# Subtract the row mean and square: stores issued from ScalarE's queue, and tiles of consecutive rows instead of interleaved ones

## The chip, the core and the metric

The kernel runs on one core of one Trainium2 chip. Of the core's engines it uses VectorE (DVE in the profile), ScalarE (ACT), SyncE (SP, which only issues transfers here) and the 16 DMA engines that move data between HBM and the on-chip memory (SBUF, 128 partitions). The metric is the device time of one execution in microseconds (us), as a median over runs.

## The reference

The input `x` is a float32 array of 1024 rows of 4096 elements; the axis is the last one.

```python
mean = np.mean(x, axis=axis, keepdims=True)
return ((x - mean) ** 2).astype(np.float32)
```

So every row is reduced to its mean, the mean is subtracted, and each element is squared. 16.78 MB are read and 16.78 MB are written.

## The kernel before

The work is cut into two tiles. A tile holds 512 rows: each of the 128 partitions holds four whole rows (`Q = 4`), 16,384 floats or 64 KiB, one row behind the other. Both tiles have a buffer of their own (`bufs=ntiles`), so no load waits for a buffer.

Which rows of `x` a partition holds is set by the rearrange pattern `"(p n q) d -> n p (q d)"`: partition `p` owns the eight consecutive rows `8p` to `8p+7`; tile 0 takes the first four of each partition's eight, tile 1 the last four. In HBM, the 64 KiB run of one partition in one tile therefore starts 128 KiB after that of the partition before it. The output is laid out in the same way.

All loads are issued first, on SP's queue (line 51): for tile 0 a short head of 512 columns and then the remaining 15,872 columns, for tile 1 one transfer of the whole tile.

Then the tiles are worked on one after the other, all in place in `x_tile`:

- ScalarE takes the mean of row 3 with an activation that also accumulates (line 59, `mean_on_act`), then the squares: row 3, row 0, row 1 and the first 2304 columns (`H`) of row 2 (line 74, `square_on_act`, with the negated mean as the bias).
- VectorE takes the means of rows 0, 1 and 2 (line 67 a reduction, line 70 the scaling by 1/4096), and then the last 1792 columns of row 2: an addition of the negated mean (line 89) and a multiplication with itself (line 90).
- One store of the whole tile (8 MiB) is issued at line 91, on SP's queue, where it waits for VectorE's line 90 and for ScalarE's last square.

`inorder` (`tc.keep_in_program_order`) pins an instruction behind what was traced before it on its engine. The reductions, the scalings and the squares are pinned in this way; the activation of line 59, the lines 89 and 90 and the transfers are not, and are placed by the scheduler of the tile framework from their data and their order in the program. Line 122 is the end of the program: SP waits there for all transfers.

Of the kernel before, what the change touches and what calls it, by code (L numbers as in the profile page):

```python
# [2 lines left out]

os.environ.setdefault("NEURON_RT_ULTRASERVER_MODE", "4")

# [4 lines left out]

F32 = mybir.dt.float32
ACT = mybir.ActivationFunctionType


@with_exitstack
def kernel(
    ctx: ExitStack,
    tc: tile.TileContext,
    x: bass.AP,
    axis: bass.AP,  # L20
    out: bass.AP,
):

    nc = tc.nc

    B, D = x.shape  # L30
    P = nc.NUM_PARTITIONS
    Q = 4
    HEAD = 512
    H = D * 9 // 16
    assert B % (P * Q) == 0
    ntiles = B // (P * Q)
    inv_d = 1.0 / float(D)

    x_t = x.rearrange("(p n q) d -> n p (q d)", p=P, q=Q)
    out_t = out.rearrange("(p n q) d -> n p (q d)", p=P, q=Q)  # L40

    io = ctx.enter_context(tc.tile_pool(name="io", bufs=ntiles))
    scratch = ctx.enter_context(tc.tile_pool(name="scratch", bufs=1))
    stats = ctx.enter_context(tc.tile_pool(name="stats", bufs=2 * ntiles * Q))

    tiles = []
    for i in range(ntiles):
        x_tile = io.tile([P, Q * D], F32)
        cuts = [0, HEAD, Q * D] if i == 0 else [0, Q * D]
        for lo, hi in zip(cuts, cuts[1:]):  # L50
            nc.sync.dma_start(out=x_tile[:, lo:hi], in_=x_t[i][:, lo:hi])  # L51
        tiles.append(x_tile)

    inorder = tc.keep_in_program_order

    def mean_on_act(row):
        copy = scratch.tile([P, D], F32)
        neg_mean = stats.tile([P, 1], F32)
        nc.scalar.activation(  # L59
            out=copy, in_=row, func=ACT.Identity, scale=-inv_d, accum_out=neg_mean  # L60
        )
        return neg_mean

    def mean_on_dve(row):
        neg_sum = stats.tile([P, 1], F32)
        neg_mean = stats.tile([P, 1], F32)
        inorder(nc.vector.reduce_sum(  # L67
            out=neg_sum, in_=row, axis=mybir.AxisListType.X, negate=True
        ))
        inorder(nc.vector.tensor_scalar_mul(out=neg_mean, in0=neg_sum, scalar1=inv_d))  # L70
        return neg_mean

    def square_on_act(part, neg_mean):
        inorder(nc.scalar.activation(  # L74
            out=part, in_=part, func=ACT.Square, bias=neg_mean, scale=1.0
        ))

    for i in range(ntiles):
        row = [tiles[i][:, q * D:(q + 1) * D] for q in range(Q)]
        m3 = mean_on_act(row[3])  # L80
        m0 = mean_on_dve(row[0])
        square_on_act(row[3], m3)
        m1 = mean_on_dve(row[1])
        square_on_act(row[0], m0)
        m2 = mean_on_dve(row[2])
        square_on_act(row[1], m1)
        square_on_act(row[2][:, :H], m2)
        back = row[2][:, H:]
        nc.vector.tensor_scalar_add(out=back, in0=back, scalar1=m2)  # L89
        nc.vector.tensor_mul(out=back, in0=back, in1=back)  # L90
        nc.sync.dma_start(out=out_t[i], in_=tiles[i])


# [1 line left out]
_INS = ['x', 'axis']  # L95
_OUTS = [((1024, 4096), 'float32')]

_NUMBERS = {'axis': -1}


# [26 lines left out]
```

## Time and profile before

| what | us |
|---|---|
| median of 3 runs | 83.14 |
| lowest and highest of them | 82.9 and 83.14 |
| the profiled execution's own time | 83.14 |
| its span in the profile | 81.4 |
| DVE busy | 33.4 |
| ACT busy | 34.7 |
| the 16 DMA engines busy, share of the span | 95.9% |

The span runs from the first to the last instruction of the profiled execution; what lies between the span and the execution's own time (83.14 - 81.4) is outside the profile. Busy times are summed over an engine's instructions. The share of the DMA engines is a mean over all 16 of them. The profile's queue `q1` is the one hardware queue that all five transfers of this kernel use, since all are issued from SP.

The traced transfers are cut into packets: 128 of 2 KiB (the head), 128 of 63,488 bytes (the rest of tile 0's load) and 384 of 64 KiB (tile 1's load and the two stores), and 80 of 4 bytes (one at the end of each of the five transfers on each of the 16 engines). Every large packet is one partition's run, so each DMA engine moves eight of them for each transfer.

### The profile page before, as it was taken

Reading aid. Unit: us, or ns where it says so; the run is one execution under the profiler, and the core shown is the slowest. Engines: PE = TensorE matmul, PEld = TensorE weight load, DVE = VectorE, ACT = ScalarE, POOL = GpSimd, SP = SyncE. Lnnn points to the kernel's source line nnn. Section 1 sums busy time; section 2 is a strip of 40 time slices with the busy share of each in tenths; the row PEclk is TensorE's granted clock in tenths of the full one; section 3 lists DMA queues with packets and bytes.
Section 4 is the critical chain, followed back from the end, with each engine's and each line's share of the span. In section 5 each row is a group of like instructions: output and inputs, shape, how many; then the busy total and the mean of one; then the engine's idle time right before and its main releaser. Section 6 shows DMA issues by size and latency. Waiting matters only on the chain.

```text
span 81.4 us, 83 instructions
## 1 busy us (share of the span) xinstructions
DVE 33.4 (41%) x16; ACT 34.7 (43%) x13; POOL 0.2 (0%) x4
## 2 busy tenths in 40 slices
DVE  0000000000089999999439999999900000000000
ACT  6000000000099999999339999999800000000000
POOL 0000000000000000000000000000000000000000
DMA  1999939999992999993899998399999199999290
GB/s 26 602 499 468 406 156 468 499 499 499 516 451 97 483 516 516 516 483 161 387 516 516 516 483 387 161 516 516 516 516 451 64 516 516 516 516 483 129 419 0
DMA packets 720, 33.55 MB, mean 412 GB/s; under 512 B 80, under 2 KB 80, under 8 KB 208
## 3 DMA queue, kind: packets, MB, share of 16 engines
q1 hardware_dynamic: 720, 33.55, 95.9%
HBM read 16.78 MB, written 16.78 MB: 412 GB/s over the span
## 4 chain that ended last, share of the span: by engine, by line
DMA 49%; DVE 21%; SPq 1%; issue 0%
DMA x_tile<-in_x_dram 49%; DVE neg_sum L67 16%; DVE x_tile L90 2%; DVE x_tile L89 1%; SPq L51 1%; DVE neg_mean L70 1%
## 5 line engine op out<-in xcount | busy, mean ns | idle before, releaser
L67 DVE TENSOR_REDUCE neg_sum<-x_tile 128x1 f32<-128x4096 f32 x6 | 26.5, 4412 | 25.0 <-DMA x_tile<-in_x_dram 25.0
L74 ACT ACTIVATE x_tile<-x_tile,neg_mean 128x4096 f32<-128x4096 f32 (+1 forms) x8 | 26.0, 3324 | 0.1
L59 ACT ACTIVATE copy<-x_tile 128x4096 f32<-128x4096 f32 x2 | 7.2, 3617 | 23.1 <-DMA x_tile<-in_x_dram 23.1
L90 DVE TENSOR_TENSOR x_tile<-x_tile 128x1792 f32<-128x1792 f32 x2 | 4.1, 2026 | 0.1
L89 DVE TENSOR_SCALAR x_tile<-x_tile,neg_mean 128x1792 f32<-128x1792 f32 x2 | 2.3, 1153 | 0.1
L59 ACT ACT_TABLE_LOAD x1 | 1.3, 1283 | 0.7 <-PEq L108 0.7
L70 DVE TENSOR_SCALAR neg_mean<-neg_sum 128x1 f32<-128x1 f32 x6 | 0.9, 154 | 0.2
L59 ACT ACTIVATION_READ_ACCUMULATOR copy<-x_tile 128x1 f32 x2 | 0.4, 186 | 0.0
L108 POOL MEMSET const-bfloat16-1.0<- 128x1 bf16 x1 | 0.1, 102 | 0.0
L108 POOL MEMSET const-uint8-127<- 128x1 uint8 x1 | 0.1, 101 | 0.0
L108 POOL MEMSET const-float32-0.0<- 128x1 f32 x1 | 0.1, 99 | 0.2 <-issue 0.2
L108 POOL MEMSET const-float32-1.0<- 128x1 f32 x1 | 0.1, 98 | 0.0
## 6 DMA issues: line engine op xcount, KB each, us to landing
x_tile<-in_x_dram SPq DMA_DIRECT2D x1, 7936.0 KB, 21.4
x_tile<-in_x_dram SPq DMA_DIRECT2D x1, 256.0 KB, 2.6
out_dram<-x_tile SPq DMA_DIRECT2D x2, 21.7
x_tile<-in_x_dram SPq DMA_DIRECT2D x1, 40.2
```

What stands on the lines that cost most here:

```text
L51: nc.sync.dma_start(out=x_tile[:, lo:hi], in_=x_t[i][:, lo:hi])
L59: nc.scalar.activation(out=copy, in_=row, func=ACT.Identity, scale=-inv_d, accum_out=neg_mean)
L67: inorder(nc.vector.reduce_sum(out=neg_sum, in_=row, axis=mybir.AxisListType.X, negate=True))
L70: inorder(nc.vector.tensor_scalar_mul(out=neg_mean, in0=neg_sum, scalar1=inv_d))
L74: inorder(nc.scalar.activation(out=part, in_=part, func=ACT.Square, bias=neg_mean, scale=1.0))
L89: nc.vector.tensor_scalar_add(out=back, in0=back, scalar1=m2)
L90: nc.vector.tensor_mul(out=back, in0=back, in1=back)
L108: nc = _bacc.Bacc("TRN2", target_bir_lowering=False, num_devices=1)
```

## The change

The rows that a partition owns are dealt out in another way, and the store is issued from another engine:

- In `"(n p q) d -> n p (q d)"` tile 0 is the first 512 rows of `x` and tile 1 the last 512. Partition `p` holds rows `4p` to `4p+3` of its tile, and the runs of neighbouring partitions follow each other in HBM without a gap: 64 KiB apart instead of 128 KiB. A whole tile is one block of 8 MiB. The output is laid out in the same way. Sizes and counts of transfers, the order of the loads, and what the engines compute stay as they are.
- The store of a tile is issued by `nc.scalar.dma_start`, on ScalarE's queue, instead of by `nc.sync.dma_start`. In the program it stands behind ScalarE's last square of that tile and ahead of its first activation of the next one. The loads stay on SP's queue.

An empty line falls away as well, so line numbers behind it are smaller by one in the new file.

```diff
@@ -24,7 +24,6 @@
-
     nc = tc.nc
...
-    x_t = x.rearrange("(p n q) d -> n p (q d)", p=P, q=Q)
-    out_t = out.rearrange("(p n q) d -> n p (q d)", p=P, q=Q)
+    x_t = x.rearrange("(n p q) d -> n p (q d)", p=P, q=Q)
+    out_t = out.rearrange("(n p q) d -> n p (q d)", p=P, q=Q)
...
         nc.vector.tensor_scalar_add(out=back, in0=back, scalar1=m2)
         nc.vector.tensor_mul(out=back, in0=back, in1=back)
-        nc.sync.dma_start(out=out_t[i], in_=tiles[i])
+        nc.scalar.dma_start(out=out_t[i], in_=tiles[i])
```

## The prediction

> **What bounds the kernel now.** I read the page's engine lines first, then its DMA lines, then the chain of waits, and then the timeline and the transfer windows around the two places where a store is issued. The page, busy times and DMA:
>
> ```profile
> DVE 33.4 (41%) x16; ACT 34.7 (43%) x13; POOL 0.2 (0%) x4
> q1 hardware_dynamic: 720, 33.55, 95.9%
> ```
>
> No compute engine is busy for half the span; the 16 DMA engines are for 95.9% of it. The chain of waits, in order of time, with the lines between left out:
>
> ```profile
> 1.64 40.24 DMA x_tile<-in_x_dram
> ...
> 56.76 2.02 DVE x_tile L90
> ```
>
> The chain runs through the loads to 41.88, through tile 1's computation to 58.78, and what is left of the span belongs to the last store: 21.7 us from its issue to its landing. That looks like load, compute, store in a row, but the DMA engines never rest meanwhile. Windows over the transfers show it. A packet is booked at its start, so GB/s times the length, divided by 65,536 bytes, is the number of 64 KiB packets that start in a window. The columns: window, length, DVE, ACT, POOL busy, clock, DMA share, GB/s.
>
> ```profile
> 38.30:39.20 0.90, 0.90 (x1) 0.90 (x1) 0.00 (x0) 1.00 2.70 1165
> 39.20:40.80 1.60, 0.30 (x1) 0.09 (x1) 0.00 (x0) 1.00 0.00 0
> 40.80:41.05 0.25, 0.00 (x0) 0.00 (x0) 0.00 (x0) 1.00 1.22 524
> 41.05:41.60 0.55, 0.00 (x0) 0.00 (x0) 0.00 (x0) 1.00 3.86 1668
> 41.60:43.20 1.60, 1.30 (x1) 1.30 (x1) 0.00 (x0) 1.00 0.00 0
> ...
> 60.30:60.90 0.60, 0.00 (x0) 0.00 (x0) 0.00 (x0) 1.00 4.05 1748
> ...
> 77.20:77.80 0.60, 0.00 (x0) 0.00 (x0) 0.00 (x0) 1.00 4.03 1748
> 77.80:80.30 2.50, 0.00 (x0) 0.00 (x0) 0.00 (x0) 1.00 0.00 0
> ```
>
> At 38.3 to 39.2 all 16 engines start their last packet of tile 1's load; at 40.8 to 41.6 (2 packets, then 14) they start the first of store 0; at 60.3 to 60.9 the first of store 1; at 77.2 to 77.8 the last of all. The trace's packet records give the rest. A 64 KiB packet takes 2.418 us in the median (27.1 GB/s on one engine), read or written, 2.487 at worst; a 63,488-byte one takes 2.342 us once the stream runs, but the first on each engine takes up to 2.994. The first packet starts at 1.74, the last ends at 80.21, and no engine stands idle for over 0.39 us in all between. One engine's load is 8 head packets (0.90 us, their mean sum), 8 x 2.342 and 24 x 2.418: 77.7 us, of the 78.5 there are. The DMA engines are the bound, and no reordering of the same bytes can take much from it. A change of over 0.3%, 0.25 us, is about what a measurement of this kernel can tell from none.
>
> **Part 1, the rows.** Removed and added: nothing in counts. The five transfers, their packets and their sizes stay; only HBM addresses move, from a pitch of 128 KiB to 64 KiB. The trace has no packet at the new pitch. The nearest rows are the 384 packets at the old one: reads and writes both at 2.418 us, so HBM isn't what limits a packet now, and I take zero. Above: if the packets of one direction all took the worst steady time, 2.487, that is 16 x 0.069 = +1.1 us; of both directions, +2.2 us. Below: steady packets show no stall that could go, but the start does. The engines come out of the head and their first large packet spread out, and that spread lasts to the end: in the last transfer the earliest engine ends at 79.67, the last at 80.21. If the new addresses let all start as the best do, -0.54 us.
>
> A rule weighed against that row stands in the Trainium skill, page "DMA: Bandwidth & Descriptors", section "Latency and other measured facts": copies with a large power-of-two pitch between the partitions' rows lose rate (207 GB/s per direction at 512 KiB, 103 at 4 MiB, 214 with a pad), and it advises contiguous tiles. Its smallest pitch is four times the one here; taken at its word for 512 KiB, the 3% between 207 and 214 would be an estimated gain of some 2.6 us and 80.5 us. The row of 2.418 us leaves no room for that.
>
> **Part 2, the store's queue.** Two DMA issues (0.35 us each on SP) go from SP's queue to ACT's, with their two waits on VectorE. Both issue places in the timeline:
>
> ```profile
> 37.47 2.03 DVE L90 TENSOR_TENSOR x_tile<-x_tile 128x1792 f32<-128x1792 f32 x1
> 39.56 0.35 SPq L91 DMA_DIRECT2D out_dram<-x_tile  x1
> 41.90 3.62 ACT L59 ACTIVATE copy<-x_tile 128x4096 f32<-128x4096 f32 x1 [2.61 <-DMA x_tile<-in_x_dram]
> ...
> 58.85 0.34 SPq L91 DMA_DIRECT2D out_dram<-x_tile  x1
> ```
>
> *The wait.* ACT ends its last square of tile 0 at 39.29, VectorE ends line 90 at 39.50. ACT now stands 0.2 us at the wait and issues at 39.56 as SP did. Behind it on ACT is tile 1's line 59, which waits for tile 1's load until 41.90 anyway: 41.90 - 39.56 - 0.35 = 2.0 us of cover. If the load landed earlier than that, each issue of 0.35 us would lie on ACT's path. In tile 1 nothing is queued behind the store but the end of the program, where SP waits for the landing as before. On SP nothing useful stood behind the stores. Cost: 0.
>
> *The start.* No issue from ACT is in this trace. From the issue to the first packet it took 41.04 - 39.56 = 1.48 us for the store, and 1.74 - 0.73 = 1.01 us for the first load, so one issue can differ from another by 0.47 us. How much of a delay shows? The engine that finishes last is free for store 0 at 41.58 and for store 1 at 60.90, while first packets can start at 41.04 and, at the same distance from the issue, at 60.33: 0.54 us of slack. Both stores shift alike, and store 1's issue doesn't depend on store 0, so a delay of d costs max(0, d - 0.54) once. For d I take 0 to 0.47, the nearest rows: cost 0. At the upper end a whole second start, 1.48 us, costs 0.94. An earlier start gains nothing, because the engines are still busy with the load.
>
> *The order between queues.* On one queue store 0's packets stood behind tile 1's load; on two queues nothing says so. But when the first store packet can start, at 41.04, each engine has long begun its last load packet (all between 38.3 and 39.2): there is none left to overtake. The margin is 41.04 - 39.2 = 1.8 us. If the store came earlier than that, one packet of it on every engine would push the load's landing by 2.42 us, and with it store 1's start from 60.33 to 62.75, behind the 60.90 at which the last engine falls free: +1.85 us.
>
> The rule that speaks against the change is on the same page of the skill, section "Queues, rings and completion order": each DMA engine takes turns between the queues that have work, packet by packet. This trace, with one queue, can't show it; by it, two queues cost 0 within that margin and the same 1.85 us outside it.
>
> **The sum.** Rows 0, wait 0, start 0, order 0. Against the profiled execution's own 83.14 us (span 81.4 and 1.7 around it), which is also the median of the runs shown: 83.1.
>
> **The rivals.**
>
> *ACT starts transfers later* (slower). For it: every issue in the trace is SP's, and 0.54 us is little. Against: issues differ by 0.47 at most here. It decides from d = 0.54 on; 0.79 is needed for 0.25 us; at d = 1.48, 84.1 us.
>
> *The 64 KiB pitch disturbs HBM* (slower). For it: first packets of up to 2.994 us show that packets can be held up. Against: 384 packets without a stall. One direction at the worst steady row: 83.14 + 1.1 = 84.2; both: 85.3.
>
> *Tile 1's mean goes ahead of store 0 on ACT* (slower). Line 59 isn't pinned by `inorder`, so the program doesn't force the store before it. Then ACT would stand at the load until 41.90 and issue no sooner: first packets at 41.90 + 1.48 = 43.38, 1.8 us after the last engine falls free, 84.9 us; if the issue also waits for the activation's end, 3.6 us more. Against: the store comes first in the program and its wait ends 2.4 us before the load lands.
>
> *A smoother start* (faster). For it: the spread of 0.54 us and a head that takes until 2.67 to 3.02. Against: nothing says that the new addresses do better. 82.6 us, and no source beyond it: the whole difference between the 78.5 us and one engine's 77.7 us of packets is 0.8.
>
> **How the numbers follow.** Forecast of no change 0.42; late start 0.17, disturbed HBM 0.17, wrong order 0.06, together 0.40 slower; smoother start 0.18. The slower cases get as much together because each has a bound above its slack and none a row of its own here. The range goes from the smoother start, 82.6, to one direction disturbed, 84.2, each widened by half the spread of the runs shown (0.12): 82.5 to 84.4. Left out are the wrong order and part of the disturbed case, some 0.15. The forecast's own range is 82.9 to 83.4.
>
> **What would show it.** Right: a second hardware queue with half the bytes, still near 96% for both together; bursts of 16 packets every 2.42 us from 3 to 80; the store's issue at 39.6 on ACT's queue, line 59 of tile 1 behind it at 41.9; the second issue at 58.9. Wrong: an empty stretch in the DMA line after 41 or 60 (late start, or the order, by where ACT's issue stands against line 59); packets of over 2.43 us (HBM); a landing of tile 1's load after 42.5 (queues overtaking).

## The result, and the profile after

The changed kernel takes 83.88 us in the median of 6 runs (83.82 to 83.98), the kernel before 83.09 in 6 runs beside it: ratio 1.0096, 95% interval 1.008 to 1.0113. It is slower by 0.8 us. Its profiled execution took 83.98 us, with a span of 82.2.

The page of the changed kernel, the engines and the DMA queues (packets, MB, share of the 16 engines' span):

```profile
DVE 33.4 (41%) x16; ACT 34.7 (42%) x13; POOL 0.2 (0%) x4
q10 hardware_dynamic: 288, 16.78, 48.1%
q1 hardware_dynamic: 432, 16.78, 48.0%
```

The engines do the same work in the same time. The bytes are now split between two queues, and the shares add up to 96.1% of a longer span: the DMA engines count as busy for longer (0.961 x 82.2 = 79.0 us against 0.959 x 81.4 = 78.1) with the same bytes. So no idle stretch was added; packets must have become longer. The issues, with the time to landing, and the place of the first store in the timeline:

```profile
out_dram<-x_tile ACTq DMA_DIRECT2D x2, 22.5
```

```profile
37.50 2.03 DVE L89 TENSOR_TENSOR x_tile<-x_tile 128x1792 f32<-128x1792 f32 x1
39.61 0.38 ACTq L90 DMA_DIRECT2D out_dram<-x_tile  x1
41.91 3.62 ACT L58 ACTIVATE copy<-x_tile 128x4096 f32<-128x4096 f32 x1 [2.59 <-DMA x_tile<-in_x_dram]
...
58.88 0.34 ACTq L90 DMA_DIRECT2D out_dram<-x_tile  x1
```

Store 0 is issued at 39.61 (39.56 before), line 58 of tile 1 follows it at 41.91 (41.90 before), store 1 is issued at 58.88 (58.85). Up to here the two executions agree within 0.05 us, and yet a store needs 22.5 us to land instead of 21.7. The transfer windows show where. In them the DMA share of a packet is booked at its start, so where a window holds one start on each of the 16 engines, share times length is the mean time of those packets. The columns are those of the windows in the prediction.

```profile
38.60:39.20 0.60, 0.60 (x1) 0.60 (x1) 0.00 (x0) 1.00 4.03 1748
39.20:41.00 1.80, 0.32 (x1) 0.11 (x1) 0.00 (x0) 1.00 0.00 0
41.00:41.60 0.60, 0.00 (x0) 0.00 (x0) 0.00 (x0) 1.00 5.45 1748
41.60:44.30 2.70, 2.39 (x1) 2.39 (x1) 0.00 (x0) 1.00 0.00 0
44.30:44.80 0.50, 0.50 (x1) 0.50 (x1) 0.00 (x0) 1.00 4.84 2097
61.20:61.70 0.50, 0.00 (x0) 0.00 (x0) 0.00 (x0) 1.00 4.85 2097
78.10:78.60 0.50, 0.00 (x0) 0.00 (x0) 0.00 (x0) 1.00 4.84 2097
```

The last load packets take 4.03 x 0.60 = 2.42 us, the first packets of store 0 take 5.45 x 0.60 = 3.27, the second ones (44.3) 4.84 x 0.50 = 2.42 again, and the first of store 1 (61.2) and the last of all (78.1) too. One packet on each engine is 0.85 us too long, all 16 at the same place, and everything behind it is late by that: the last packet ends at 80.99 instead of 80.22. The packet records, which give start, length, size and queue but not the engine, add a detail that decided the experiments: each of these long packets (3.09 to 3.47 us) starts within 6 ns of the start of one of the load's closing 4-byte records, so with no gap behind the load. The store's packets seem to have been there in time: they waited for a busy engine, and then ran long.

The **loss** below is this sum for a kernel: the time of the large packets that start between 27 and 48 us above their due (2.418 us for 64 KiB, 2.342, 1.815, 1.213 and 0.611 for the smaller sizes), divided by the 16 engines. It is 0.02 us before and 0.85 after.

### The profile page after: what moved, and what is told of

The parts are those of the page before. It is cut to its first block, busy times and chain, and to the rows that moved or that the text cites. A ratio compares the mean times of both kernels' runs of the same rounds, so it can differ in the third digit from the quotient of the medians.

```text
span 82.2 us, 82 instructions
## 1 busy us (share of the span) xinstructions
DVE 33.4 (41%) x16; ACT 34.7 (42%) x13; POOL 0.2 (0%) x4
## 4 chain that ended last, share of the span: by engine, by line
DMA 49%; DVE 20%; SPq 1%; issue 0%
DMA x_tile<-in_x_dram 49%; DVE neg_sum L66 16%; DVE x_tile L89 2%; DVE x_tile L88 1%; SPq L50 1%; DVE neg_mean L69 1%
## 6 DMA issues: line engine op xcount, KB each, us to landing
out_dram<-x_tile ACTq DMA_DIRECT2D x2, 22.5
```

## The experiments

A time that stands without a ratio is that of a single execution; the others are medians of 4 to 12, and the ratio is to the kernel before, run beside them.

### One half of the change at a time

Store on ScalarE's queue, rows as before:

```diff
-        nc.sync.dma_start(out=out_t[i], in_=tiles[i])
+        nc.scalar.dma_start(out=out_t[i], in_=tiles[i])
```

> The rows of before, both stores on ScalarE's queue. In the changed kernel the first packet of store 0 on each engine took 3.09 to 3.47 us where a 64 KiB packet takes 2.418; the second store paid nothing. If the queue is the cause (first use of it, a switch between queues, or a late start), this kernel shows the same: first packets of store 0 near 3.2 us, about +0.8 us, 83.9. If the rows are the cause (the first writes at the new pitch), first packets near 2.42 and 83.1.

Measured: 83.85 us, ratio 1.0103 (1.0085 to 1.0121), loss 0.83 us. The windows of this kernel:

```profile
40.90:41.40 0.50, 0.00 (x0) 0.00 (x0) 0.00 (x0) 1.00 6.46 2097
```

6.46 x 0.50 = 3.23 us for the first store packets. The queue alone brings the whole difference. One of the 16 tells more: on it the store packet starts 0.18 us behind the closing record (41.19 to 41.38) and takes 2.468 us; the other 15 follow the load without a gap and take 3.09 to 3.47. (A later expectation puts this gap at 48 ns; that pairs the packet with a closing record that another store packet follows by 6 ns.)

The rows alone:

```diff
-    x_t = x.rearrange("(p n q) d -> n p (q d)", p=P, q=Q)
-    out_t = out.rearrange("(p n q) d -> n p (q d)", p=P, q=Q)
+    x_t = x.rearrange("(n p q) d -> n p (q d)", p=P, q=Q)
+    out_t = out.rearrange("(n p q) d -> n p (q d)", p=P, q=Q)
```

> The rows of the change, both stores on SP's queue. If the queue is the cause of the 0.8 us: 83.1, first packets of store 0 near 2.42 us. If the rows are: 83.9 and first packets near 3.2 us.

Measured: 83.15 us, ratio 1.0014 (1.0000 to 1.0027), loss 0.01. The first packets of store 0:

```profile
41.00:41.70 0.70, 0.00 (x0) 0.00 (x0) 0.00 (x0) 1.00 3.47 1498
```

They take 3.47 x 0.70 = 2.43 us. The rows are not the cause. They cost at most a trace: in seven of the ten kernels with these rows, the changed one among them, the fifth packet of tile 0's load on each engine takes 2.38 to 2.47 us in the median where 2.342 is due; with the rows of before it never does.

### First use, or every change of queue?

The head load of the changed kernel on ScalarE's queue too:

```diff
-            nc.sync.dma_start(out=x_tile[:, lo:hi], in_=x_t[i][:, lo:hi])
+            eng = nc.scalar if hi == HEAD else nc.sync
+            eng.dma_start(out=x_tile[:, lo:hi], in_=x_t[i][:, lo:hi])
```

> The changed kernel with the short head load (256 KB) on ScalarE's queue too, so that this queue has moved packets on all 16 engines before store 0. First use of a queue as the cause: store 0's first packets near 2.42 us, and some 0.8 us less than the changed kernel, about 83.1. A switch between queues or a late start from ScalarE: first packets near 3.2 us as before, 83.9. The head and the main load are then issued side by side, which may move the start of the stream by up to 0.4 us either way; so the packets of store 0 decide, not the total alone.

Measured: 83.51 us, ratio 1.0058 (1.0045 to 1.0071), loss 0.05. Store 0's first packets took 2.45 to 2.47 us. That looks like first use; but they start after gaps, of about 0.1 to 0.2 us, and the next kernel contradicts it. The 0.5 us by which this kernel is still slower than the one before are largely at its start: the first large packets of the load, behind a head on another queue, take 3.06 us in the median instead of 2.58 with the rows alone. Store 0 from ScalarE, store 1 from SP:

```diff
-        nc.sync.dma_start(out=out_t[i], in_=tiles[i])
+        (nc.scalar if i == 0 else nc.sync).dma_start(out=out_t[i], in_=tiles[i])
```

> The rows of before, store 0 on ScalarE's queue and store 1 on SP's. A cost at each switch between queues: store 1 goes back to SP's queue and its first packets take near 3.2 us too, 84.7. First use, or a late start from ScalarE: only store 0 pays, 83.9. The rows as cause: 83.1.

Measured: 84.62 us, ratio 1.0191 (1.0178 to 1.0205): twice the loss. Its windows at the two hand-overs:

```profile
40.90:41.40 0.50, 0.00 (x0) 0.00 (x0) 0.00 (x0) 1.00 6.54 2097
61.00:61.50 0.50, 0.00 (x0) 0.00 (x0) 0.00 (x0) 1.00 6.35 2097
```

3.27 us for the first packets of store 0, and 3.18 for those of store 1, which goes back to SP's queue, used since the start of the kernel. First use is out, and so is a slow start that belongs to ScalarE.

### One queue again, but ScalarE's

```diff
-            nc.sync.dma_start(out=x_tile[:, lo:hi], in_=x_t[i][:, lo:hi])
+            nc.scalar.dma_start(out=x_tile[:, lo:hi], in_=x_t[i][:, lo:hi])
...
-        nc.scalar.activation(
+        inorder(nc.scalar.activation(
             out=copy, in_=row, func=ACT.Identity, scale=-inv_d, accum_out=neg_mean
```

> The changed kernel with its three loads on ScalarE's queue as well (and line 58 pinned, so that the stores keep their place): one queue again, but ScalarE's. If the cost lies in going over from one queue to another: store 0's first packets near 2.42 us, about 83.1 (the rows alone measured 83.15). If anything that ScalarE issues while the engines are busy starts slowly: first packets near 3.2 us, 83.9. The loads are issued in front of the activation table, which shifts nothing on the path as the first data come 20 us later.

Measured: 83.09 us, ratio 1.0004 (0.9991 to 1.0017), loss 0.01. The first store packets take 2.42 to 2.46 us, in the mean 3.04 x 0.80 = 2.43:

```profile
41.00:41.80 0.80, 0.00 (x0) 0.00 (x0) 0.00 (x0) 1.00 3.04 1311
```

With everything on one queue the change costs nothing, whoever issues.

### A busy engine or an idle one?

Store 1 of the kernel with the two hand-overs, held back:

```diff
+        for _ in range(4 if i == 1 else 0):
+            nc.vector.tensor_scalar_add(out=back, in0=back, scalar1=0.0)
         (nc.scalar if i == 0 else nc.sync).dma_start(out=out_t[i], in_=tiles[i])
```

> The rows of before, store 0 on ScalarE's queue, store 1 on SP's, and store 1 held back by four more additions of zero on VectorE (1.15 us each, 4.6 us), so that the engines stand idle when it arrives at about 64.5 (store 0 ends near 61.4). In the kernel without the delay store 1's first packets took 2.96 to 3.33 us. If every change of queue costs: first packets near 3.2 us again. If it costs only where the new queue's packets already wait while the engine is still on the old queue's last packet: near 2.46 us, as the one engine that had a gap of 48 ns before store 0 (2.468) suggests. Total about 84.6 + 3.3 = 87.9 in the one case, 87.1 in the other.

Measured: 86.54 us. The windows:

```profile
40.90:41.40 0.50, 0.00 (x0) 0.00 (x0) 0.00 (x0) 1.00 6.53 2097
61.00:64.00 3.00, 2.09 (x2) 0.00 (x0) 0.00 (x0) 1.00 0.00 0
64.00:64.30 0.30, 0.00 (x0) 0.00 (x0) 0.00 (x0) 1.00 8.19 3495
```

Store 0 pays as ever (3.27). No packet starts from 61 to 64, and store 1's first packets take 8.19 x 0.30 = 2.46 us: the same change of queue, but to idle engines, costs 0.04. The total is below both expected values, because the packets came 0.84 us after the issue (63.21 to 64.05), not the 1.5 that I had assumed.

The opposite: store 0 earlier, with packets of the load still to come. The first kernel leaves out tile 0's squares of rows 1 and 2, the second one also has the head on ScalarE's queue.

```diff
-        square_on_act(row[1], m1)
-        square_on_act(row[2][:, :H], m2)
...
+        if i == 1:
+            square_on_act(row[1], m1)
+            square_on_act(row[2][:, :H], m2)
...
```

> The changed kernel without tile 0's squares of row 1 and of row 2, on either engine (left out: those outputs of tile 0 are x itself), so that store 0 is issued on ScalarE's queue near 33.6 instead of 39.6, with two or three packets of tile 1's load left on each engine. Turns between the queues: store packets go in between the load's last ones and tile 1's load lands near 41.9 + 4.8 = 46.7 or later. One queue after the other: the load lands at 41.9. A cost at each turn: every one of these alternating packets takes near 3.2 us; a cost once, when an engine first turns to the waiting queue: only the first store packet does.

> The same with the head load on ScalarE's queue, so that the queue has been used before. In the kernel with the head there and the store at its usual place, store 0's first packets took 2.45 to 2.47 us, but each engine stood idle for 0.04 to 0.2 us before them. If earlier use of the queue is what saved the 0.8 us: first store packets near 2.42 us here as well. If the idle engine is what saved it: near 3.2 us, as the queue now waits for a busy engine.

Measured: losses of 1.13 and 1.01 us, totals of 88.20 and 88.15. The windows of the first, five waves of 16 packets:

```profile
33.80:34.40 0.60, 0.60 (x1) 0.00 (x0) 0.00 (x0) 1.00 4.04 1748
36.30:36.80 0.50, 0.00 (x0) 0.00 (x0) 0.00 (x0) 1.00 7.08 2097
39.70:40.30 0.60, 0.00 (x0) 0.00 (x0) 0.00 (x0) 1.00 4.03 1748
42.10:42.70 0.60, 0.00 (x0) 0.00 (x0) 0.00 (x0) 1.00 4.03 1748
44.50:45.10 0.60, 0.00 (x0) 0.00 (x0) 0.00 (x0) 1.00 4.03 1748
```

The store was issued at 33.60. The wave at 33.8 still takes 2.42 us, the wave at 36.3 takes 3.54, and by the packet records both are load packets, on the old queue. The next waves are store, load, store, all at 2.42. So it is neither the new queue's packet that is slow nor each turn: each engine loses about 1 us once, on the first packet that it starts more than 0.7 us after the store's issue. Earlier use of the queue doesn't help. And the queues do take turns: the load lands at 47.88 instead of 41.88, two store packets of 2.42 and the loss later. The Trainium skill, page "DMA: Bandwidth & Descriptors", section "Queues, rings and completion order", says that an engine takes turns between its queues packet by packet; this trace agrees.

Store 0 of the changed kernel held back by a little:

```diff
+        if i == 0:
+            bit = row[2][:, H:H + 512]
+            nc.vector.tensor_scalar_add(out=bit, in0=bit, scalar1=0.0)
         nc.scalar.dma_start(out=out_t[i], in_=tiles[i])
```

> The changed kernel with store 0 held back by one more addition of zero to 512 columns on VectorE, some 0.4 us, so that it is issued near 40.0 instead of 39.6. If packets lose 0.8 us where they wait for a busy engine and nothing where they reach an idle one, a part of the engines is idle by then: their first packets take near 2.46 us after a gap of 0.05 to 0.4, the others near 3.2 us, and the later issue is faster than the changed kernel: 83.4 to 83.8. If the start is simply late: 0.4 us later, 84.3.

Measured: 83.91 us, ratio 1.0096 (1.0072 to 1.0120). Here the expected gain is missing, and the packets say why:

```profile
41.20:41.60 0.40, 0.00 (x0) 0.00 (x0) 0.00 (x0) 1.00 5.78 2458
41.60:41.70 0.10, 0.00 (x0) 0.00 (x0) 0.00 (x0) 1.00 2.05 655
```

15 packets (2458 x 0.40 / 65.5) of 5.78 x 0.40 x 16 / 15 = 2.47 us, and one, on the engine that was last to finish the load, of 2.05 x 0.10 x 16 = 3.28. The 15 had gaps of 0.17 to 0.22 us before them (closing records and store packets paired in order of time), the one had none. The loss is 0.11 us in the mean over engines, but the last engine sets the end. So with 1024 columns in place of 512:

```diff
-            bit = row[2][:, H:H + 512]
+            bit = row[2][:, H:H + 1024]
```

> The changed kernel with store 0 held back by an addition of zero to 1024 columns, so that it is issued near 40.4 (39.6 in the changed kernel, 40.2 with 512 columns). If the packets lose 0.8 us only where they wait for a busy engine, nearly all engines now stand idle for 0.1 to 0.3 us when they arrive, and no first packet or at most one takes over 3 us: 83.2 to 83.5, less than the changed kernel's 83.9. If one engine still pays: 83.9. If later is simply later: 84.6.

Measured: 83.46 us, ratio 1.0029 (0.9999 to 1.0059). Its first store packets:

```profile
41.20:41.80 0.60, 0.00 (x0) 0.00 (x0) 0.00 (x0) 1.00 4.10 1748
```

Store 0 is issued at 40.35, 0.74 us later than in the changed kernel; all first packets take 2.45 to 2.47 (in the mean 4.10 x 0.60 = 2.46); and the kernel is 0.4 us faster than the changed one, whose ratio was 1.0096 (1.008 to 1.0113). It doesn't beat the kernel before.

### The rival order

Tile 1's first activation ahead of store 0 on ScalarE:

```diff
         m3 = mean_on_act(row[3])
+        if i == 1:
+            inorder(nc.scalar.dma_start(out=out_t[0], in_=tiles[0]))
```

> The changed kernel with tile 1's line 58 ahead of store 0 on ScalarE, the rival order of the prediction, priced there at 84.9. Issued near 42.0 the store reaches idle engines: first packets near 2.46 us, starting 1.0 to 2.0 us after the issue (43.0 to 44.0) where the last load packet ends at 41.6, so the last engine is 2.3 us late and 85.3 follow if its start is the latest, 84.6 if it is not. If the issue waits for the activation's end at 45.6: 88.5.

Measured: 84.70 us, ratio 1.0195 (1.0166 to 1.0224), loss 0.05. The store is issued at 41.97, while the activation runs; its first packets start at 42.84 to 42.99, 0.87 to 1.02 us later, and take 2.46. Here the cost is a plain idle stretch.

### What in the transfer sets the loss

The store in halves:

```diff
-        nc.scalar.dma_start(out=out_t[i], in_=tiles[i])
+        for lo in (0, Q * D // 2):
+            hi = lo + Q * D // 2
+            nc.scalar.dma_start(out=out_t[i][:, lo:hi], in_=tiles[i][:, lo:hi])
```

> The changed kernel with each store cut into two of half the columns, so that a store packet has 32 KiB and takes 1.21 us. The first packet of store 0 on each engine took 3.24 us where 2.418 is due. A fixed loss for each engine: 1.21 + 0.82 = 2.03 us now, about 83.9 in all. A loss in proportion to the packet: 1.34 x 1.21 = 1.62 us, about 83.5.

Measured: 84.41 us, ratio 1.0156 (1.0125 to 1.0186). It doesn't answer the question: the first half needs only rows 0 and 1, so it was issued at 37.23 already, and the loss (1.06 us) fell on the load's last 64 KiB packets. With the turns between the queues the load landed at 44.24, but that is not what made the total longer: the DMA engines were idle for 0.3 us each, against 0.2 in the changed kernel. The loss is 0.2 us larger; the rest of the 0.5 I can't name.

A small extra load on ScalarE's queue in the kernel before, first with one packet of 512 bytes on each engine, then with eight:

```diff
         square_on_act(row[0], m0)
+        if i == 0:
+            tiny = scratch.tile([16, 128], F32)
+            inorder(nc.scalar.dma_start(out=tiny, in_=x[0:16, 0:128]))
```

```diff
+            tiny = scratch.tile([P, 128], F32)
+            inorder(nc.scalar.dma_start(out=tiny, in_=x[0:P, 0:128]))
```

> The kernel before, with all its transfers on SP's queue, and one more load of 8 KB (16 partitions of 512 bytes, one packet on each engine, read by nobody) on ScalarE's queue behind its second square of tile 0, near 30, in the middle of tile 1's load. If a second queue costs each busy engine some 0.8 to 1.1 us once, whatever it carries: one packet near 31 to 36 on each engine takes 3.2 to 3.6 us, tile 1's load lands near 42.8, 83.9 to 84.1. If the loss belongs to the large store: 83.1 to 83.2.

> The kernel before and a small extra load (128 partitions of 512 bytes, eight packets on each engine, read by nobody) on ScalarE's queue in the middle of tile 1's load. If the count of packets that wait on the second queue sets the loss: one 64 KiB packet on each engine takes 3.0 to 3.8 us between 29 and 35, and 83.9 to 84.2. If their size or the direction does: all near 2.42 to 2.5 us, and 83.1 to 83.4 (the extra packets themselves 8 x 0.03 us).

Measured: 83.22 us, ratio 1.0003 (0.9986 to 1.0021), for the one; 83.12, loss 0.00, for the other. A second queue as such costs nothing, nor do eight packets of 512 bytes. Then one packet of 32 KiB on each engine, in 16 partitions (the tile is `[16, 2 * D]`):

> The same with one packet of 32 KiB on each engine (16 partitions, 512 KB in all). If the size of the waiting packet sets the loss: one packet on each engine takes 0.6 to 1.4 us longer than its due (2.418, or 1.21 for the new one), and 83.1 + 1.2 + 0.9 = 85.2. If count or direction: no such packet, 84.3.

Measured: 88.54 us. The extra packets took 2.99 to 4.67 us instead of 1.21, and the load packets behind them 3.2 to 4.9. That is more than any theory here gives: a loss of 4.2 us by 39, before any store was issued (39.48). All these packets write to 16 neighbouring partitions, which no other transfer does but the one of 512 bytes; whether that is why was not tested, so this run stands against the others as an open exception. Last, two transfers of eight packets of 16 KiB on each engine that differ in direction (and in the issue, at 30.10 and 27.08), row 3 of tile 0 as a store of its own, and 128 whole rows of `x` as an extra load:

```diff
+        if i == 0:
+            inorder(nc.scalar.dma_start(out=out_t[0][:, 3 * D:], in_=row[3]))
...
-        nc.sync.dma_start(out=out_t[i], in_=tiles[i])
+        hi = (3 if i == 0 else 4) * D
+        nc.sync.dma_start(out=out_t[i][:, :hi], in_=tiles[i][:, :hi])
```

```diff
+        if i == 0:
+            extra = scratch.tile([P, D], F32)
+            inorder(nc.scalar.dma_start(out=extra, in_=x[0:P, :]))
```

> The kernel before with row 3 of tile 0 stored by itself, on ScalarE's queue behind the second square (near 30), the other three rows and tile 1 on SP's: a store of eight packets of 16 KiB on each engine. The turns between the queues push the landing of tile 1's load by 8 x 0.6 = 4.8 us in any case, to 46.7, and store 1's issue with it to 63.7, where the engines fall free at 60.9: some 86 to 86.5. If a store, or several large packets, set the loss: one packet on each engine near 30 to 34 takes 0.6 to 1.4 us more than its due, and 87. If only 64 KiB packets do: none.

> The kernel before and an extra load of 2 MB (128 partitions of 16 KiB, eight packets on each engine, read by nobody) on ScalarE's queue in the middle of tile 1's load. If a packet's size sets the loss: the packets from 28 on take together some 1.0 us for each engine more than their due, as with the stored row of the same size. If the direction does (a store against a load): near 0. The load itself costs 8 x 0.61 = 4.9 us and pushes tile 1's landing in any case; with store 1 issued later by as much, the total comes to some 86 to 87.

Measured: row 3 as a store, 85.81 us and a loss of 0.88 us by 39, before store 0 comes, spread over several load packets of 2.5 to 3.1 us. The extra load, 89.29 us, more than the 86 to 87 expected: the DMA engines were idle for only 0.2 us each, so its 4.9 us and the loss both count in full. Its windows:

```profile
31.80:32.30 0.50, 0.50 (x1) 0.50 (x1) 0.00 (x0) 1.00 4.85 2101
...
40.80:41.40 0.60, 0.00 (x0) 0.00 (x0) 0.00 (x0) 1.00 5.65 1748
```

From 31 to 40 loads of two queues alternate, 0.61 and 2.42 us, almost without loss (4.85 x 0.50 = 2.42; 0.03 us in all). At 40.8 a wave takes 5.65 x 0.60 = 3.39, and each packet of the other queue after it 0.94 to 1.34 instead of 0.61. In between, at 39.39, SP had issued store 0, on the queue of the load that it stands behind, while ScalarE's queue was still at work. From 40.5 on the loss is 1.53 us. So in this run it came with a store, not with the second load, and came even though the store's own queue was the old one.

Taken over all hand-overs from one queue to another at which the store comes behind the last packet of a transfer of 64 KiB packets, its first packets fall into two groups, 80 in each. One takes 2.96 to 3.47 us, and each of its packets starts within 6 ns of a closing record (16 in the changed kernel, 15 with the queue alone, 32 with two hand-overs, 16 at store 0 of the kernel with store 1 held back, 1 with 512 columns). The other takes 2.44 to 2.47, and, paired with the closing records in order of time, each of its packets has a gap of 0.08 us or more before it. None lies between.

## Why the prediction was wrong

I forecast no change, 83.1 us, and put 0.42 on it; measured are 83.88, within the range of 82.5 to 84.4, on the side that had 0.40. That it lies within the range is luck: the upper end came from disturbed HBM, not from what happened. Step by step:

- **The bound** was right: the DMA engines decide, and every 0.8 us lost on each of them is 0.8 us of the time.
- **Rows, 0:** right. 1.0014 (1.0000 to 1.0027) for the rows alone. The estimate of 2.6 us of gain from the skill's row on power-of-two pitches had no place to come from, as the row of 2.418 us said; the contiguous tiles ran at 2.418 us too. The sign that I had listed for disturbed HBM, packets of over 2.43 us, did come (3.27), but from the queue: with the rows alone they took 2.43, with the queue alone 3.23.
- **The wait, 0:** right. ACT's issue took 0.38 us, at 39.61, and line 58 began at 41.91.
- **The start, 0:** right in its value, wrong in its working. Where all engines stood idle, the first packet started 0.84 to 0.88 us after the issue, from SP (63.21 to 64.05) as from ScalarE (41.97 to 42.84), and the last of the 16 within 1.02. The 1.48 us that I took from the trace of before wasn't a start: 15 of the 16 first packets began as soon as an engine had finished the load, at 41.03 to 41.58. So the slack was about 1.1 us (an estimate: 41.58 - 39.56 - 0.88), not 0.54, and "ACT starts later" was not what happened, though its price of up to 0.94 lies near the measured one.
- **The order between queues, 0: this is the step that failed.** No store packet overtook the load, as I said, and the load landed at 41.88 as before. But I took the hand-over itself as free, because in the trace of before the store follows the load without a gap. That trace has one queue. On two, a store packet that follows the load without a gap ran 0.85 us long in the mean (0.75 to 0.87 at such hand-overs; 0.88 to 1.13 for each engine in mid-stream). It should have stood in the sum as an operation that the trace doesn't show, with a bound of its own; the long first packets of the load (up to 2.994 us, against 2.342) were a row that would have given one, +0.65.
- **Outside the margin** I priced one overtaking packet at 2.42 us. With the store at 33.60 the load landed 6.0 us late: two packets and the loss.
- **The wrong order** was priced at 84.9 and measured at 84.70. The last engine's idle stretch was 1.4 us, not 1.8, for the same reason as the start.
- **A smoother start** didn't show: in the changed kernel the spread between the engines was 0.45 us at the end, against 0.54.

## What to carry to other kernels

Where the DMA engines are the bound, as here, try first to issue a store that follows a load without a gap on the queue that the load is on; in this kernel moving it to another engine's queue saved nothing and cost 0.8 us at each hand-over. "The new packet can't overtake anything" doesn't make a second queue free. And a time to first packet is a start only if the DMA engines were idle before it; next to a busy engine it measures the engine.

## What the runs showed of the hardware

- A store that comes while the engines are at work on another queue cost each of them 0.75 to 1.13 us once (1.53 us where two loads ran side by side), unless they had a gap before its first packet. It shows on the next packet or, with 16 KiB packets, spread over several, whichever queue these are on. The kernels that share this: store on ScalarE's queue behind loads on SP's, store on SP's behind a store on ScalarE's, store on SP's behind SP's load while ScalarE's load runs.
- Without loss were: all on one queue (0.01 to 0.02, from SP or ScalarE), an idle engine (2.46 us, so 0.04), loads of two queues side by side once they run (0.00 to 0.03, at 512 bytes and 16 KiB; the load of 32 KiB packets into 16 partitions is the exception, with 4.2).
- Later can be faster: issued 0.74 us later, store 0 made the changed kernel 0.4 us faster (83.46).
- Open: what the engine does in that time, and how long before its last packet's end a store must arrive to cost it. With the head on ScalarE's queue an engine that finished the load 1.77 us after the store's issue had a gap of 0.2 us and lost nothing more; in the changed kernel engines that finished 1.43 to 1.93 us after it lost 0.7 to 1.05. So "busy when the store comes" is the condition that fits, not one that is shown to be enough; what the traces show without exception is the gap. No run here separates the two.
